# Head sums of a hybrid attention and recurrence layer: two float32r passes over high and low parts instead of one float32 product

## The chip, the core and the metric

The kernel runs on one core of a Trainium2 chip. The metric is the device time of one execution in microseconds (us). The core has a matmul engine (TensorE, "PE"), a vector engine (VectorE, "DVE"), a scalar engine for activation functions (ScalarE, "ACT"), GpSimd ("POOL") and SyncE ("SP"), which here issues the DMAs. Each works through its own queue in order; semaphores make one wait for another. Matmul results go to PSUM, all else lies in SBUF.

## What is computed

One layer over x of 512 positions by 1024 features, all in float32:

```
x = x + 0.5 * SwiGLU1(rmsnorm(x))            1024 -> 2816 -> 1024
p = rmsnorm(x) @ W_in
  q, k, v     8 heads of 64: stick-breaking attention, q and k rms-normalised per head,
              its output rms-normalised per head
  r, k, v, ..  8 heads of 64: RWKV-7 recurrence; its k is normalised per head, its output
              is group-normalised per head, plus the bonus sum(r * kf * r_k) * v
x = x + concat(o_sb, o_rw) @ W_out
x = x + 0.5 * SwiGLU2(rmsnorm(x))
```

Five times in it a sum over the 64 features of one head is wanted at every position: the mean square of q and of k (qm), the norm of the recurrence's k (kn), the bonus (bn), the variance of the recurrence's output (var), and the mean square of the attention's output (om).

## The kernel before

Features lie on the 128 partitions and the 512 positions along the free dimension, so that one [128, 512] tile holds a pair of heads. There are four pairs, j = 0 to 3, in the recurrence and four in the attention. Weights and activations are split into a float32r high part and a float32r rest, and `mm3` (L176) makes a float32 product of three float32r passes.

Three parts follow each other: FFN 1 (to about 370 us), the mixing stage, and FFN 2 (from about 763 us). The mixing stage has

- dense items on the shared list `stream` (L755): for each pair, projections K, R, V (recurrence) and Q (q or k of the attention), two SV for the attention's v; last PR(j), the output projection for pair j of both halves, eight groups of six matmuls each into "wo", added to x;
- three chains per pair. I(j), `rw_inverse`: blocks A, a small triangular inverse on VectorE with two trips through DRAM, three transposing blocks (tB, tA, W0), then seven products "inv" with copies between them, MG and N. C(j), `rw_chain`: six steps S, each waiting for the last; then y, the variance var, the gate g and the output orw. T(j), `att_core`: four steps of growing width (128 to 512), each z on PE, three activations per head, a scan and two other operations on VectorE, transposes wT, an exponential, and o; then the sum om.

A planner (L788) asks for these pieces in an order by estimated costs. The framework's scheduler then orders each engine's instructions by priority (C 3000, I 500, T none, L750) and by its own estimate of when inputs are ready. Tiles of one tag share a fixed number of buffers (`NB`, L97 for SBUF, `NM` for PSUM), which are handed out in the order in which the program asks for them: "r" has 10 and holds most of the recurrence's tiles; PSUM tag "mi" has 2 banks, used by I and by the y, var and g of C; "ma" has 3, used by T.

The sums over a head's 64 rows are made by `head_sum` (L200): a float32 matmul with the block matrix "blk" of the constants, which puts the sum over each head's rows on all of these rows. Its input is a square made by ScalarE (or the product `xr` for bn). There are 24: qm 8, kn 4, bn 4, om 4, var 4.

Of the kernel before, what the change touches and what calls it, by code (L numbers as in the profile page):

```python
# [16 lines left out]
F32 = mybir.dt.float32  # L17
# [65 lines left out]
def layer(ctx, tc, a, out, dbg=None):  # L83
# [10 lines left out]
        uid[0] += 1  # L94
        return f"{s}_{uid[0]}"

    NB = {"x": 16, "q": 3, "b": 4, "r": 10, "i": 10, "c": 6, "v": 4, "k": 4, "g": 8, "a": 4, "t": 2, "f": 4, "s": 2}  # L97
    NM = {"acc": 2, "sd": 1, "mi": 2, "ma": 3}
    NW = 3

# [47 lines left out]
    def cs(n):  # L148
        return cst[:, CST[n][0]:CST[n][1]]
# [47 lines left out]
    def norm_in(g):  # L197
        return [split(X[k], "x", v(g, k), "x") for k in range(KD)]

    def head_sum(ps, x):  # L200

        nc.tensor.matmul(ps, lhsT=cs("blk"), rhs=x, start=True, stop=True)

    def norm_scale(want_e=False, eng=nc.gpsimd):
        tot = None
# [136 lines left out]
    def eye():  # L342
        z = slot("i", "Z")
        nc.gpsimd.tensor_scalar(c3(z), cs("i64").unsqueeze(1).to_broadcast([P, NCH, CH]), 1.0, None, MUL)
        return z

    xs = norm_in("nmx")
    pwa = dense(a["wrw"][12], xs, "wa")
    S, rs, E = norm_scale(True)
# [56 lines left out]
    def item_k(j):  # L406

        ps = dense(a["wrw"][4 + j], xs, "k")
        yield
        xk = shifted(ps, 4 + j, "r", "xk")  # L410
        sq = slot("r", "ksq")
        act(sq, xk, AF.Square, scale=v("kk", j))
        pn = bank("sd", "kn")
        head_sum(pn, sq)
        nc.vector.tensor_scalar(sq, pn, 1e-24, None, MAX)
        act(sq, sq, AF.Ln)
        act(sq, sq, AF.Exp, scale=-0.5)
        kn = slot("r", "kkn")
        nc.vector.scalar_tensor_tensor(kn, xk, v("kk", j), sq, MUL, MUL)

        kf = slot("r", "kf")
        nc.vector.tensor_scalar(kf, av[j], v("ka", j), oka[:, j:j + 1], MUL, ADD)
        nc.vector.tensor_tensor(kf, kf, xk, MUL)
        ctxs[j] = dict(kn=kn, kf=kf)

    def item_r(j):

        ps = dense(a["wrw"][j], xs, "r")
        yield
        kn, kf = ctxs[j]["kn"], ctxs[j]["kf"]  # L430
        xr = shifted(ps, j, "r", "xr")
        Pd = slot("r", "Pd")
        act(Pd, Gs[j], AF.Exp, scale=-KAPPA)
        PC = small([P, NCH], "PC", 4)
        nc.gpsimd.tensor_scalar(PC.unsqueeze(2), c3(Pd)[:, :, CH - 1:CH], 1.0, None, MUL)
        AR = quad("AR")
        ar = c3(AR, P)
        nc.vector.scalar_tensor_tensor(ar[:, :, 1:CH], c3(kn)[:, :, 1:CH], -1.0, c3(Pd)[:, :, 0:CH - 1], MUL, MUL)
        nc.vector.tensor_scalar(ar[:, :, 0:1], c3(kn)[:, :, 0:1], -1.0, None, MUL)
        nc.vector.tensor_tensor(ar[:, :, CH:P], c3(xr), c3(Pd), MUL)  # L440
        nc.vector.scalar_tensor_tensor(xr, xr, v("rk", j), kf, MUL, MUL)
        pbn = bank("sd", "bn")
        head_sum(pbn, xr)
        bv = ctxs[j]["xv"]
        nc.vector.tensor_tensor(bv, pbn, bv, MUL)

        Pi = slot("r", "Pi")
        act(Pi, Gs[j], AF.Exp, scale=KAPPA)
        BK = quad("BK")
        bk = c3(BK, P)  # L450
        nc.vector.tensor_tensor(kn, kn, av[j], MUL)
        for src, q in ((kn, 0), (kf, 1)):
            for p, eng in ((0, nc.vector), (1, nc.gpsimd)):
                o_ = slice(CH * (q ^ p), CH * (q ^ p) + CH)
                eng.tensor_tensor(bk[rows[p], :, o_], c3(src[rows[p]]), c3(Pi[rows[p]]), MUL)
        ctxs[j].update(PC=PC, AR=AR, BK=BK, bv=bv)
# [153 lines left out]
    def rw_chain(j):  # L610

        js = slice(j * P, (j + 1) * P)
        PC, ar, ba, bv, UV, St = (ctxs[j][n] for n in ("PC", "ar", "ba", "bv", "UV", "St"))
        for c in range(1, NCH - 1):
            cc = slice(c * CH, (c + 1) * CH)
            nn = slice((c + 1) * CH, (c + 2) * CH)
            pS = bank("mi", "S", [P, CH])
            for p in range(2):
                nc.tensor.matmul(pS[rows[p]], lhsT=ar[rows[p], c, 0:CH], rhs=St[rows[p], cc], start=True, stop=True)
            nc.vector.scalar_tensor_tensor(St[:, nn], pS, PC[:, c:c + 1], St[:, nn], MUL, ADD)  # L620
            yield 1.2

        py = bank("mi", "y")
        for c in range(NCH):
            cc = slice(c * CH, (c + 1) * CH)
            for p in range(2):
                nc.tensor.matmul(py[rows[p], cc], lhsT=UV[p][:, cc], rhs=ba[p][:, c, CH:P], start=c == 0, stop=False)
        for c in range(1, NCH):
            cc = slice(c * CH, (c + 1) * CH)
            for p in range(2):  # L630
                nc.tensor.matmul(py[rows[p], cc], lhsT=St[rows[p], cc], rhs=ar[rows[p], c, CH:P],
                                 start=False, stop=c == NCH - 1)

        yc = slot("r", "yc")
        nc.scalar.copy(yc, py)
        yr = slot("r", "yr")
        act(yr, py, AF.Square)
        pv = bank("mi", "var")
        head_sum(pv, yr)
        act(yr, pv, AF.Ln, scale=1.0 / CH, bias=epsl)  # L640
        act(yr, yr, AF.Exp, scale=-0.5)
        nc.vector.scalar_tensor_tensor(yr, yc, v("lnw", j), yr, MUL, MUL)
        nc.vector.scalar_tensor_tensor(yr, yr, v("lnb", j), bv, ADD, ADD)
        pg = bank("mi", "g")
        nc.tensor.matmul(pg, lhsT=g2[:, js], rhs=sgx, start=True, stop=True)
        o = slot("g", "orw")
        nc.vector.tensor_tensor(o, pg, yr, MUL)
        outs[4 + j] = o
        yield 5
# [17 lines left out]
    def item_qk(j, e):  # L667

        ps = dense(a["wqk"][4 * e + j], xs, "qk"[e])
        yield  # L670
        qc = slot("k", "qc")
        nc.scalar.copy(qc, ps)
        ps = qc
        rn = slot("k", "rn")
        act(rn, ps, AF.Square, scale=CH ** -0.5)
        pm = bank("sd", "qm")
        head_sum(pm, rn)
        nc.vector.tensor_tensor(rn, pm, E, ADD)
        act(rn, rn, AF.Ln)
        act(rn, rn, AF.Exp, scale=-0.5)  # L680
        nc.vector.scalar_tensor_tensor(rn, ps, v("kn") if e else gq8, rn, MUL, MUL)
        ctxs["qk", j, e] = rn

    def att_core(j):
        qh, kh = ctxs["qk", j, 0], ctxs["qk", j, 1]
        po = bank("ma", "o")
        for i in range(4):
            L = (i + 1) * P
            pz = [bank("ma", "z") for _ in range(2)]
            for p in range(2):  # L690
                nc.tensor.matmul(pz[p][:, 0:L], lhsT=qh[rows[p], i * P:L], rhs=kh[rows[p], 0:L], start=True, stop=False)  # L691
            for p in range(2):
                nc.tensor.matmul(pz[p][:, i * P:L], lhsT=ninf, rhs=mkb, start=False, stop=True)
            ws = []
            for p in range(2):
                l = slot("a", "l")
                act(l[:, 0:L], pz[p][:, 0:L], AF.Abs)
                act(l[:, 0:L], l[:, 0:L], AF.Exp, scale=-1.0)
                act(l[:, 0:L], l[:, 0:L], AF.Ln, bias=1.0)
                r = slot("a", "r")  # L700
                nc.vector.tensor_scalar(r[:, 0:L], pz[p][:, 0:L], 0.0, None, MAX)
                nc.vector.tensor_tensor_scan(l[:, 0:L][:, ::-1], r[:, 0:L][:, ::-1], l[:, 0:L][:, ::-1], 0.0, ADD, ADD)
                nc.vector.tensor_tensor(r[:, 0:L], pz[p][:, 0:L], l[:, 0:L], SUB)
                ws.append(r)
            yield 2 + i
            ats = []
            for p in range(2):
                pt = bank("ma", "wT")
                for b in range(i + 1):
                    nc.tensor.transpose(pt[:, b * P:(b + 1) * P], ws[p][:, b * P:(b + 1) * P], cs("ident"))  # L710
                at = slot("t", "at")
                act(at[:, 0:L], pt[:, 0:L], AF.Exp)
                ats.append(at)
            for b in range(i + 1):
                for p in range(2):
                    hd = 2 * j + p
                    nc.tensor.matmul(po[rows[p], i * P:L], lhsT=Vt[b][:, hd * CH:(hd + 1) * CH],  # L717
                                     rhs=ats[p][:, b * P:(b + 1) * P], start=b == 0, stop=b == i)
            yield 2
        rn = slot("t", "orn")  # L720
        act(rn, po, AF.Square, scale=CH ** -0.5)
        pm = bank("ma", "om")
        head_sum(pm, rn)
        act(rn, pm, AF.Ln, bias=epsr)
        act(rn, rn, AF.Exp, scale=-0.5)
        o = slot("s", "osb")
        nc.vector.scalar_tensor_tensor(o, po, v("son", j), rn, MUL, MUL)
        outs[j] = o
        yield 4
# [146 lines left out]
```

## Time and profile before

| what | value |
|---|---|
| three timed runs | 1135.84, 1137.49, 1137.58 us |
| profiled execution, its own time | 1135.56 us |
| its span | 1133.8 us |
| PE busy | 1105.7 us (98%) |
| DVE, ACT, POOL busy | 567.3, 445.6, 182.6 us |

The span is what the profiler sees between the first and the last instruction; some 1.8 us lie around it. A matmul of 512 columns is listed with about 0.39 us, but these overlap: the next one starts 0.23 us later. So PE's busy time is read for gaps, not as work. A float32 matmul is two instructions in the trace, each 0.59 us when listed.

### The profile page before, as it was taken

Reading aid. Unit: us, or ns where it says so; the run is one execution under the profiler, and the core shown is the slowest. Engines: PE = TensorE matmul, PEld = TensorE weight load, DVE = VectorE, ACT = ScalarE, POOL = GpSimd, SP = SyncE. Lnnn points to the kernel's source line nnn. Section 1 sums busy time; section 2 is a strip of 40 time slices with the busy share of each in tenths; the row PEclk is TensorE's granted clock in tenths of the full one; section 3 lists DMA queues with packets and bytes.
Section 4 is the critical chain, followed back from the end, with each engine's and each line's share of the span. In section 5 each row is a group of like instructions: output and inputs, shape, how many; then the busy total and the mean of one; then the engine's idle time right before and its main releaser. Section 6 shows DMA issues by size and latency. Waiting matters only on the chain.

```text
span 1133.8 us, 16807 instructions
## 1 busy us (share of the span) xinstructions
PE 1105.7 (98%) x6499; PEld 870.7 (77%) x6499; DVE 567.3 (50%) x966; ACT 445.6 (39%) x782; POOL 182.6 (16%) x135
## 2 busy tenths in 40 slices
PE   8999999999999998999999998999999999999998
PEld 6888888888888766866677665777888888888887
DVE  7444443443333466487777777674434444433322
ACT  6333333333323553364644654553333333322221
POOL 1111111120001233221311312041111111110000
PEclk9999999999999999999999999998999999999999
DMA  5332333233333224311302102022333232334442
GB/s 203 100 96 93 102 93 102 93 90 102 99 93 104 90 66 112 88 47 40 75 27 53 39 23 57 11 74 93 93 101 96 94 102 93 103 90 116 115 114 68
DMA packets 67231, 97.79 MB, mean 86 GB/s; under 512 B 19280, under 2 KB 21456, under 8 KB 67152
## 3 DMA queue, kind: packets, MB, share of 16 engines
q1 hardware_dynamic: 67152, 96.73, 29.0%
q8 instruction: 51, 0.84, 0.3%
q14 instruction: 28, 0.23, 0.1%
HBM read 93.03 MB, written 3.67 MB: 85 GB/s over the span
## 4 chain that ended last, share of the span: by engine, by line
PE 87%; DVE 8%; ACT 2%; issue 1%; DMA 1%; SPq 0%; DVEq 0%; ACTq 0%
PE g L179 7%; PE g L178 7%; PE g L177 7%; PE dn L178 7%; PE dn L177 7%; PE u L179 7%; PE dn L179 7%; PE u L177 7%; PE u L178 7%; PE inv L566 2%; PE z L691 2%; PE o L717 1%; PE k L177 1%; PE k L179 1%; PE k L178 1%
## 5 line engine op out<-in xcount | busy, mean ns | idle before, releaser
L162 ACT CAST wh<-w 128x512 fp32r<-128x512 f32 (+1 forms) x315 | 192.1, 610 | 412.9 <-PE dn L178 146.6
L163 DVE TENSOR_TENSOR wl<-w,wh 128x512 fp32r<-128x512 f32 (+1 forms) x294 | 200.2, 681 | 246.4 <-ACT wh L162 245.7
L179 PE MATMUL g<-xh,wl 128*128 128x512 f32 x352 | 138.1, 392 | 1.9 <-DVE wl L163 1.9
L177 PE MATMUL u<-xh,wh 128*128 128x512 f32 x352 | 137.2, 390 | 2.6 <-ACT wh L162 2.6
L178 PE MATMUL g<-xl,wh 128*128 128x512 f32 x352 | 138.1, 392 | 0.7 <-DVE xl L193 0.7
L177 PE MATMUL g<-xh,wh 128*128 128x512 f32 x352 | 138.2, 393 | 0.1
L179 PE MATMUL u<-xh,wl 128*128 128x512 f32 x352 | 137.1, 390 | 0.0
L178 PE MATMUL u<-xl,wh 128*128 128x512 f32 x352 | 137.1, 389 | 0.0
L302 POOL TENSOR_TENSOR h<-sg,u 128x512 f32<-128x512 f32 x44 | 69.1, 1571 | 395.8 <-DVE u L300 386.2
L177 PE MATMUL dn<-hdh,wh 128*128 128x512 f32 x240 | 93.4, 389 | 0.0
L178 PE MATMUL dn<-hdl,wh 128*128 128x512 f32 x240 | 93.4, 389 | 0.0
L179 PE MATMUL dn<-hdh,wl 128*128 128x512 f32 x240 | 93.4, 389 | 0.0
L179 PEld LDWEIGHTS g<-xh,wl 128*128 128x128 f32 x352 | 66.8, 190 | 16.2 <-DVE wl L163 2.3
L177 PEld LDWEIGHTS u<-xh,wh 128*128 128x128 f32 x352 | 66.1, 188 | 17.1 <-ACT wh L162 3.3
L178 PEld LDWEIGHTS g<-xl,wh 128*128 128x128 f32 x352 | 66.6, 189 | 15.0 <-DVE xl L193 1.1
L177 PEld LDWEIGHTS g<-xh,wh 128*128 128x128 f32 x352 | 66.7, 189 | 14.7 <-ACT sq L134 0.5
L178 PEld LDWEIGHTS u<-xl,wh 128*128 128x128 f32 x352 | 66.2, 188 | 13.7
L179 PEld LDWEIGHTS u<-xh,wl 128*128 128x128 f32 x352 | 66.1, 188 | 13.6
L300 DVE TENSOR_TENSOR u<-u,S 128x512 f32<-128x512 f32 x44 | 30.4, 691 | 65.7 <-PE u L179 65.7
L163 POOL TENSOR_TENSOR wl<-w,wh 128x512 fp32r<-128x512 f32 x22 | 30.4, 1384 | 137.6 <-ACT wh L162 102.6
L177 PEld LDWEIGHTS dn<-hdh,wh 128*128 128x128 f32 x240 | 45.1, 188 | 9.4
L179 PEld LDWEIGHTS dn<-hdh,wl 128*128 128x128 f32 x240 | 45.1, 188 | 9.3
(268 smaller groups left out, 1798.6 us busy)
## 6 DMA issues: line engine op xcount, KB each, us to landing
w<-wgu SPq DMA_DIRECT2D x176, 256.0 KB, 2.6
w<-wd SPq DMA_DIRECT2D x80, 256.0 KB, 2.6
w<-wrw SPq DMA_DIRECT2D x28, 256.0 KB, 2.6
w<-wqk SPq DMA_DIRECT2D x16, 256.0 KB, 2.6
wv<-wv SPq DMA_DIRECT2D x16, 256.0 KB, 2.6
wo<-wo SPq DMA_DIRECT2D x16, 256.0 KB, 2.6
x<-xT SPq DMA_DIRECT2D x8, 256.0 KB, 5.4
w<-wd SPq DMA_DIRECT2D x16, 128.0 KB, 2.0
```

What stands on the lines that cost most here:

```text
L162: cp(hi[:, :n], raw[:, :n])
L163: pool.tensor_tensor(lo[:, :n], raw[:, :n], hi[:, :n].bitcast(F32), SUB)
L177: mms.append(nc.tensor.matmul(ps, lhsT=lh, rhs=rh, start=start, stop=False))
L178: nc.tensor.matmul(ps, lhsT=lh, rhs=rl, start=False, stop=False)
L179: nc.tensor.matmul(ps, lhsT=ll, rhs=rh, start=False, stop=stop)
L300: nc.vector.tensor_tensor(u, pu, S, MUL)
L302: nc.gpsimd.tensor_tensor(h, sg, u, MUL)
L566: nc.tensor.matmul(ps[rows[p], cc], lhsT=l_[rows[p], cc], rhs=r[rows[p], cc], start=True, stop=True)
L691: nc.tensor.matmul(pz[p][:, 0:L], lhsT=qh[rows[p], i * P:L], rhs=kh[rows[p], 0:L], start=True, stop=False)
L717: nc.tensor.matmul(po[rows[p], i * P:L], lhsT=Vt[b][:, hd * CH:(hd + 1) * CH], rhs=ats[p][:, b * P:(b + 1) * P], start=b == 0, stop=b == i)
```

## The change

Every head sum takes a rounded copy of its input (`hi`, float32r), the exact rest (`lo`, made on GpSimd), and two float32r matmuls into the same bank. For the four kinds that sum a square, ScalarE computes the square twice, once in float32 and once rounded to float32r; for bn it copies. The block matrix is copied once to a float32r tile. The two parts live in a new tag "h" of two buffers; tag "r" goes from 10 buffers to 8. The variance now squares the copy yc in SBUF instead of y in PSUM.

```diff
-    NB = {"x": 16, "q": 3, "b": 4, "r": 10, "i": 10, ... "s": 2}
+    NB = {"x": 16, "q": 3, "b": 4, "r": 8, "i": 10, ... "s": 2, "h": 2}
...
-    def head_sum(ps, x):
-
-        nc.tensor.matmul(ps, lhsT=cs("blk"), rhs=x, start=True, stop=True)
+    def head_sum(ps, x, again):
+
+        hi = slot("h", "hsh", F32R)
+        again(hi)
+        lo = slot("h", "hsl", F32R)
+        nc.gpsimd.tensor_tensor(lo, x, hi.bitcast(F32), SUB)
+        nc.tensor.matmul(ps, lhsT=blk, rhs=hi, start=True, stop=False)
+        nc.tensor.matmul(ps, lhsT=blk, rhs=lo, start=False, stop=True)
+
+    def square_sum(ps, src, tag, s, scale=1.0):
+
+        x = slot(tag, s)
+        act(x, src, AF.Square, scale=scale)
+        head_sum(ps, x, lambda hi: act(hi, src, AF.Square, scale=scale))
+        return x
...
+    blk = pc.tile([P, P], F32R, name="blk")
+    nc.vector.tensor_copy(blk, cs("blk"))
...
-        head_sum(pbn, xr)
+        head_sum(pbn, xr, lambda hi: nc.scalar.copy(hi, xr))
...
-        yr = slot("r", "yr")
-        act(yr, py, AF.Square)
         pv = bank("mi", "var")
-        head_sum(pv, yr)
+        yr = square_sum(pv, yc, "r", "yr")
...
-        rn = slot("t", "orn")
-        act(rn, po, AF.Square, scale=CH ** -0.5)
         pm = bank("ma", "om")
-        head_sum(pm, rn)
+        rn = square_sum(pm, po, "t", "orn", CH ** -0.5)
```

The items Q and K are changed in the same way.

The number at the end of a name counts tiles in the order in which the program asks for them. On PE before, the variance of pair 1 (var_5993) stands among the dense matmuls of the last q, Q(3, 0) (q_5305), and pair 2's inverse (inv_6103) begins right behind it:

```order
L177 MATMUL q_5305<-xh_2934,wh_5326 128x512
L178 MATMUL q_5305<-xl_2935,wh_5326 128x512
L179 MATMUL q_5305<-xh_2934,wl_5327 128x512
L710 MATMUL wT_5166<-cst,r_5154 128x128 x2
L177 MATMUL q_5305<-xh_2938,wh_5326 128x512
L178 MATMUL q_5305<-xl_2939,wh_5326 128x512
L202 MATMUL var_5993<-yr_5991,cst 128x512
L645 MATMUL g_5999<-sgx_3077,g_617_2902 128x512
L566 MATMUL inv_6103<-X_6099,Aa_5725 64x64
```

In the changed kernel the same variance (var_6098, now two matmuls) stands behind the sum of attention 3 (om_5941), and pair 2's inverse (inv_6215) behind that:

```order
L206 MATMUL om_5941<-hsh_5944,blk 128x512
L207 MATMUL om_5941<-hsl_5946,blk 128x512
L206 MATMUL var_6098<-hsh_6101,blk 128x512
L655 MATMUL g_6111<-sgx_3079,g_617_2902 128x512
L207 MATMUL var_6098<-hsl_6103,blk 128x512
L578 MATMUL inv_6215<-X_6211,Aa_5827 64x64
L578 MATMUL inv_6215<-X_6211,Aa_5828 64x64
```

All dense items but the last three PR come before these rows; in the kernel before, the last dense item, Q(3, 1), and all four PR came after them. On ACT the copy of y (yc_6096) is made early, but the rounded square of it (hsh_6101) waits for the sum of attention 3 (hsh_5944):

```order
L134 ACTIVATE at_5920<-wT_5915 128x512
L134 ACTIVATE at_5927<-wT_5922 128x512
L134 ACTIVATE orn_5942<-o_5695 128x512
L134 ACTIVATE hsh_5944<-o_5695 128x512
L134 ACTIVATE hsh_6101<-yc_6096 128x512
L134 ACTIVATE orn_5942<-om_5941,epsr 128x512
L134 ACTIVATE orn_5942<-orn_5942 128x512
L134 ACTIVATE yr_6099<-var_6098,epsl 128x512
```

The copy yc_6096 stands 60-odd rows further up on ACT. At the end of the mixing stage, before, the variance of pair 3 (var_6818) lies between output matmuls of PR1 (wo_6523, wo_6531) and of attention 3:

```order
L179 MATMUL wo_6523<-osh_6491,wol_6520 128x512
L202 MATMUL var_6818<-yr_6816,cst 128x512
L645 MATMUL g_6824<-sgx_3077,g_617_2902 128x512
L710 MATMUL wT_5820<-cst,r_5805 128x128 x4
L717 MATMUL o_5593<-at_5818,Vt_3566 64x128
L177 MATMUL wo_6531<-orh_6487,woh_6519 128x512
```

Now it (var_6933) stands between pair 3's own y (y_6900) and PR3 (wo_7060), which needs it:

```order
L643 MATMUL y_6900<-AR_5433,St_6874 64x64 x14
L206 MATMUL var_6933<-hsh_6936,blk 128x512
L655 MATMUL g_6946<-sgx_3079,g_617_2902 128x512
L207 MATMUL var_6933<-hsl_6938,blk 128x512
L177 MATMUL wo_7060<-orh_7046,woh_7056 128x512
```

No dense matmul is left between the first product of pair 3's inverse and this place.

## Rows read from the trace of the kernel before

**Rows 1.** the page's first lines: span, and PE busy, its share, its instructions

```profile
span 1133.8 us, 16807 instructions
PE 1105.7 (98%) x6499; PEld 870.7 (77%) x6499; DVE 567.3 (50%) x966; ACT 445.6 (39%) x782; POOL 182.6 (16%) x135
```

**Rows 2.** busy time by stretch: PE, PEld, DVE, ACT, POOL, PE clock, DMA

```profile
400.00:687.00 287.00, 271.17 (x2537) 194.32 (x2535) 203.05 (x403) 152.20 (x288) 71.04 (x57) 0.99 0.22 58
687.00:763.30 76.30, 74.29 (x630) 53.98 (x630) 53.03 (x85) 37.42 (x74) 17.02 (x12) 0.98 0.18 48
```

**Rows 3.** the chain of waits around a head sum: start, us, what

```profile
404.63 0.23 PE v L179
404.86 0.86 PE qm L202 x2
```

**Rows 4.** groups by shape, POOL, 400:770 us: busy, mean ns, idle before

```profile
L163 POOL TENSOR_TENSOR wl<-w,wh 128x512 fp32r<-128x512 f32 x17 | 24.0, 1413 | 119.4 <-ACT wh L162 92.4 <-PE q L179 8.9 <-PE q L178 6.9
```

**Rows 5.** timeline of PE, attention 1, z of three steps: start, us

```profile
550.53 0.49 PE L691 MATMUL z<-rn,rn 64*128 64x128 f32 x4
555.72 0.70 PE L691 MATMUL z<-rn,rn 64*128 64x256 f32 x4
562.36 0.92 PE L691 MATMUL z<-rn,rn 64*128 64x384 f32 x4
```

**Rows 6.** timeline, ACT and DVE, attention 3 ending and variance 3

```profile
721.29 0.60 ACT L134 ACTIVATE l<-z 128x512 f32<-128x512 f32 x1 [3.88 <-PE z L693]
...
727.21 0.59 ACT L635 COPY yc<-y 128x512 f32<-128x512 f32 x1 [1.82 <-PE y L631]
729.58 0.69 ACT L134 ACTIVATE yr<-var,epsl 128x512 f32<-128x512 f32 x1 [0.79 <-PE var L202]
733.14 0.60 ACT L134 ACTIVATE orn<-o 128x512 f32<-128x512 f32 x1 [1.67 <-PE o L717]
734.34 0.61 ACT L189 CAST orh<-orw 128x512 fp32r<-128x512 f32 x1
734.99 1.42 DVE L190 TENSOR_TENSOR orl<-orw,orh 128x512 fp32r<-128x512 f32 x1 [0.24 <-ACT orh L189]
```

**Rows 7.** timelines and a group: inverse 0, pair 3 S, y, then A

```profile
465.98 1.15 PE L566 MATMUL inv<-X,Aa 64*64 64x64 f32 x32
479.34 1.09 PE L596 MATMUL MG<-BA,Q 64*64 64x128 f32 x16
482.45 0.33 PE L619 MATMUL S<-St,AR 64*64 64x64 f32 x4
...
718.61 0.28 DVE L620 SCALAR_TENSOR_TENSOR St<-S,PC,St 128x64 f32<-128x64 f32 x1 [1.31 <-PE S L619]
719.46 0.28 DVE L620 SCALAR_TENSOR_TENSOR St<-S,PC,St 128x64 f32<-128x64 f32 x1 [0.56 <-PE S L619]
725.06 1.15 PE L627 MATMUL y<-BA,UV 128*64 128x64 f32 x30
...
L489 PE MATMUL A<-AR,BK 64*128 64x128 f32 x128 | 13.2, 298 | 3.8 <-DVE BK L455 2.7 <-DVE BA L492 0.7 <-DVE St L620 0.4
```

**Rows 8.** timelines of POOL, DVE and PE: pair 3, from tA to inverse

```profile
667.77 1.77 POOL L529 TENSOR_SCALAR AR<-cst 128x512 f32<-128x512 f32 x1 [22.40 <-PE tA L518]
696.50 1.27 DVE L553 TENSOR_TENSOR X<-G,cst 128x512 f32<-128x512 f32 x2
697.22 1.15 PE L566 MATMUL inv<-X,Aa 64*64 64x64 f32 x32
```

**Rows 9.** timeline of PE: first z of attention 3, last output matmul

```profile
687.06 0.49 PE L691 MATMUL z<-rn,rn 64*128 64x128 f32 x4
762.77 0.40 PE L179 MATMUL wo<-osh,wol 128*128 128x512 f32 x1
```

**Rows 10.** busy time by stretch, around 428 us, columns as in rows 2

```profile
426.00:428.00 2.00, 0.39 (x6) 0.39 (x8) 2.00 (x3) 0.62 (x1) 0.41 (x1) 1.00 0.71 185
428.00:430.00 2.00, 2.00 (x16) 1.68 (x15) 0.94 (x4) 0.00 (x0) 0.00 (x0) 0.53 0.59 134
```

More of the change, by code (lines that the diff above doesn't have):

```diff
@@ L95, in nm @@
         return f"{s}_{uid[0]}"
-    NB = {"x": 16, "q": 3, "b": 4, "r": 10, "i": 10, "c": 6, "v": 4, "k": 4, "g": 8, "a": 4, "t": 2, "f": 4, "s": 2}
+    NB = {"x": 16, "q": 3, "b": 4, "r": 8, "i": 10, "c": 6, "v": 4, "k": 4, "g": 8, "a": 4, "t": 2, "f": 4, "s": 2, "h": 2}
     NM = {"acc": 2, "sd": 1, "mi": 2, "ma": 3}
@@ L410, in item_k @@
         xk = shifted(ps, 4 + j, "r", "xk")
-        sq = slot("r", "ksq")
-        act(sq, xk, AF.Square, scale=v("kk", j))
         pn = bank("sd", "kn")
-        head_sum(pn, sq)
+        sq = square_sum(pn, xk, "r", "ksq", v("kk", j))
         nc.vector.tensor_scalar(sq, pn, 1e-24, None, MAX)
@@ L673, in item_qk @@
         ps = qc
-        rn = slot("k", "rn")
-        act(rn, ps, AF.Square, scale=CH ** -0.5)
         pm = bank("sd", "qm")
-        head_sum(pm, rn)
+        rn = square_sum(pm, ps, "k", "rn", CH ** -0.5)
         nc.vector.tensor_tensor(rn, pm, E, ADD)
@@ L719, in att_core @@
             yield 2
-        rn = slot("t", "orn")
-        act(rn, po, AF.Square, scale=CH ** -0.5)
         pm = bank("ma", "om")
-        head_sum(pm, rn)
+        rn = square_sum(pm, po, "t", "orn", CH ** -0.5)
         act(rn, pm, AF.Ln, bias=epsr)
```

## The prediction

> **What bounds the kernel now.** The page comes first: TensorE (PE) is counted busy for 1105.7 of 1133.8 us [rows 1]. The two FFNs at the ends do not contain the change; everything that moves lies in the mixing stage, about 370 to 763 us. The busy time by stretch shows that PE has little slack there too: 15.8 us idle from 400 to 687 us, and 2.0 us from 687 us, where attention 3 begins, to 763 us [rows 2]. PE is kept busy because the long serial chains (I = inverse, C = chain, T = attention, one of each per head pair j) are laid beside dense projections. A chain step alone leaves PE idle; it is free only while dense work stands next to it in PE's order. So I read the order next, and the chains' own step times after that.
>
> **The passes themselves.** One float32 head sum holds PE for 0.86 us, against 0.23 us from one float32r matmul to the next [rows 3]. Two float32r passes take 0.45 us, so each of the 24 sums frees 0.41 us: 24 x 0.41 = 9.8 us. That is all there is to gain.
>
> **What each sum gets in addition.** One more ScalarE pass (0.60 us, the Square of orn [rows 6]) and a GpSimd subtraction (1.41 us, the mean of the same operation for the weights [rows 4]) stand between the input and the second pass: some 2.0 us more of latency per sum, 14 us on ScalarE and 34 us on GpSimd. Neither engine is near its limit (152 and 71 us busy of 287 [rows 2]), so as plain load I cost them at nothing where dense work stands beside the sum. The one copy of blk on VectorE is nothing.
>
> **What the order does.** This is the term that decides. The two parts of a sum take both buffers of the new tag "h", and those are handed out in the order in which the program asks for them. Thus only one head sum can be in flight, and none can pass an earlier one in the program. The program asks for pair 1's variance after attention 3's. In the kernel before, the scheduler put that variance far ahead; now it stands right behind attention 3's last sum. (With the buffers of "r" cut to 8 and nothing else changed, the sums keep the order of before but for neighbours, so it is "h" that does this.) The variance had already taken one of the two PSUM banks "mi" that the inverses use too. So I2, C2, I3 and C3 fall behind T3, when all projections are used up. What is left to cover them is the output projection (PR1 to PR3), and that waits for these very chains.
>
> I work out the stretch from T3's first z to the last output-projection matmul, as it now stands in PE's order.
> 1. T3 alone. The first two steps take 5.2 and 6.6 us from z to z [rows 5]; the third is taken as 8.5, between these and the last. The last takes 2.1 for its two z, then from the first ScalarE step on z (721.3) to the end of o (733.1) 11.8 us [rows 6], from which I take off 1.7 for VectorE's other work in it: 10.1. Sum 32.5.
> 2. T3's last sum: 0.6 + 0.6 + 1.4 + 0.4 = 3.0. Pair 1's sum then gets its buffers: another 1.4 + 0.4 and semaphores. Sum 5.0.
> 3. From that variance to PR1's first matmul: in before 729.6 to about 735.7, the end of orl, the first half of the 1.42 us row [rows 6], 6.1; now the first inverse products stand in between: 7.
> 4. I2 to pair 3's second A block, with 21 output matmuls: 21 x 0.23 = 4.8, three products at 1.08 are 3.2, two MG and N at about 1.05 are 3.1, A 3.3 (13.2 for four pairs) [rows 7], 0.3 for S, 3 of waits for VectorE: 17.7.
> 5. To pair 3's tA block, with five S steps that depend on each other: 9.
> 6. From tA to the first product of I3. The reset of AR on GpSimd starts at 667.8, I3's products at 697.2: 29.4 us [rows 8]. VectorE's X pair is held by other work for about 3 of it. I take 27; C2's variance and all of PR2 (10.9) lie inside.
> 7. I3 with nothing beside it: the first inverse took 465.98 to 482.45 = 16.5 with some dense matmuls in the way [rows 7]; I take 14. Six S at 0.85 (718.61 to 719.46): 5.1. y from 725.06 to yc at 727.2: 2.1 [rows 6, 7].
> 8. y to PR3: yc at 727.2 to the end of orl at 735.7 is 8.5 [rows 6]; plus 0.6 and 1.4, less 0.4: 10.1. PR3: 48 x 0.23 = 10.9.
>
> Sum 140.4, where before needs 687.06 to 763.0 = 75.9 [rows 9]: +64.5. Against it, T3 begins earlier, since what is now behind it is no longer before it: two variances with their g (3.4), I2's products, MG and N (10.7), six S and y (4.1), I3's A (3.3) and its three blocks of 16 small matmuls, taken as a product each (3.2), are 24.7 us [rows 3, 7]. 20 of the 24 sums are done by then (20 x 0.41 = 8.2), and 15 more output matmuls (3.4). That is 29.5 earlier; new waits of PE on the serial sums, as in om, qm, var, kn of one row (about 1.9 us apart at least, with 1 to 1.5 of other work between), take back some 4 (bounds -4 and +12). Start: -25.5.
>
> **The clock.** PE is counted busy for 0.39 us of 426 to 428, and the granted clock is then 0.53 over the next two us, which is nearly all at the lower of its two levels, 1.2 GHz [rows 10]. Steps 1, 2, 7 and 8 leave PE idle for more than half. On their paths lie about 6 us of matmuls in T3, 8 of products, and the first matmuls after each gap; I take half of such work at half clock: +6 (bounds 0 and 25). The Trainium skill ("TensorE: Matmul & The Clock Gate", section "HAM oscillation — how this bites in real kernels") says that idle between groups of matmuls sends the engine back to half rate each time. The trace agrees at this place; by the rule in full every uncovered group would run slow, which is the third rival.
>
> Net: 64.5 - 25.5 + 6 = +45.0. The profiled execution took 1135.56 us, 1.9 below the median of 1137.49 and 0.3 below the lowest of the three runs; 1135.6 + 45.0 = 1180.6, in round numbers 1181.
>
> **Bounds.** Tail 122 (T3 steps at 28, I3 as 11, step 6 fully beside PR2) to 156 (T3 as contended as before, step 6 at 29.4, 3 us more per variance); start -33 to -17; clock 0 to 25. Two ends that fall together give 1148 and 1212.
>
> **Rivals.** *The passes are what counts.* If dense work still hid all chains, the kernel would be faster by the 9.8: 1126. For it: PE busy 98% [rows 1], and the chains were hidden before. Against it: PE's order has no dense matmul between T3's last steps, nor between I3's first product and C3's variance. It decides only if those stretches total less than 10 us, and T3's steps alone are more. Chance 4%.
> *Latency, not order.* Each sum delays its reader by 2.0 us and PE has nothing to put there: 24 x 2.0 - 9.8 = +38, 1174, spread evenly over 400 to 763. For it: POOL's queue is in order, with waits for weight casts in it. Against it: in the first half, dense matmuls stand between a sum's input and its passes. Chance 8%.
> *The clock stays down from T3 on.* The exposed matmuls (T3 6, products 16, S and y 8) and about half of the 35 us of output matmuls run at half rate: +30 to +45 in place of 6, some 1205 to 1215. For it: rows 10. Against it: the mean granted clock from 687 to 763 is 0.98 in spite of such gaps [rows 2], and PR1 to PR3 are dense runs. Chance 12%.
> *The chains are shortened by emptier engines*, as nothing competes in the tail: tail 122, 1155 to 1160. Chance 13%, in my range.
>
> **Numbers.** My forecast of 1181, give or take 15, has 63%. 0.2% (2.3 us) is about what can be told from no change. Faster 4%, within 0.2% 1%, slower 95%. The range of 1150 to 1212 leaves out the first rival and the far end of the third.
>
> **What would show it.** Right: 400 to about 660 loses nothing (T3's first z near 660, not 687); then PE is busy for about 60% up to about 805, with idle that ends on ACT (var, z), POOL (hsl) and VectorE; head-sum passes of about 0.23 each; granted clock under 1.0 in several places after T3. Wrong: idle spread evenly from 400 on (second rival), or T3's first z later than 680, or dense matmuls at 1.2 GHz throughout PR1 and PR3.

## The result and the profile after

The changed kernel takes 1201.68 us (median of four runs, 1198.35 to 1207.72) against 1136.8: a ratio of 1.0577, 95% interval 1.0534 to 1.062. The forecast was 1181, in a range of 1150 to 1212. The sign and the main mechanism, the order of the sums, came out as forecast. The sum is 18 us short in the profiled execution (1198.35 against 1180.6): 14.7 of them lie in the start of T3, which the forecast had 25.5 us earlier, and 3.5 in the tail behind it. The profiled execution's page:

```profile
span 1196.5 us, 16875 instructions
PE 1126.3 (94%) x6499; PEld 884.5 (74%) x6499; DVE 574.5 (48%) x967; ACT 457.9 (38%) x806; POOL 211.7 (18%) x159
PEclk9999999999999999999899958887999999999999
```

The span is 62.7 us longer [rows 1], and the row of the clock, in 40 slices of 29.9 us, has a 5, three 8 and a 7 at 688 to 838 us, and one more 8 at 568 to 598 us; before has a single 8 in the whole row. The timeline of PE around T3 and at the end of the mixing stage:

```profile
676.26 0.49 PE L699 MATMUL z<-rn,rn 64*128 64x128 f32 x4 [1.34 <-DVE rn L689]
...
711.88 2.72 PE L725 MATMUL o<-at,Vt 128*64 128x128 f32 x16
715.84 0.50 PE L206 MATMUL om<-hsh,blk 128*128 128x512 f32 x1 [1.23 <-ACT hsh L134]
717.18 0.50 PE L207 MATMUL om<-hsl,blk 128*128 128x512 f32 x1 [0.85 <-POOL hsl L205]
717.84 0.61 PE L206 MATMUL var<-hsh,blk 128*128 128x512 f32 x1 [0.16 <-ACT hsh L134]
719.20 1.39 PE L207 MATMUL var<-hsl,blk 128*128 128x512 f32 x1
729.31 0.49 PE L177 MATMUL wo<-orh,woh 128*128 128x512 f32 x1
...
812.22 0.79 PE L177 MATMUL wo<-orh,woh 128*128 128x512 f32 x1 [4.46 <-ACT orh L189]
825.90 0.40 PE L179 MATMUL wo<-osh,wol 128*128 128x512 f32 x1
```

Pair 1's variance now follows T3's sum by 2 us, and I2, C2, I3, C3 come after it. From T3's first z to the start of the last output matmul there are 149.6 us, where before had 687.06 to 762.77, 75.7 [rows 9]: +73.9. T3 itself begins only 10.8 us earlier. That is the whole difference in two numbers, 73.9 - 10.8 = 63.1, where the spans differ by 62.7. Busy time by stretch (the columns of rows 2: length, busy time of PE, PEld, DVE, ACT, POOL, then PE clock):

```profile
400.00:676.20 276.20, 252.32 (x2063) 181.47 (x2062) 190.41 (x347) 151.09 (x289) 92.43 (x73) 0.97 0.22 60
676.20:714.70 38.50, 25.62 (x96) 13.43 (x96) 16.32 (x29) 13.99 (x33) 1.27 (x1) 0.60 0.05 14
676.20:826.30 150.10, 115.13 (x1102) 81.27 (x1102) 72.47 (x142) 50.61 (x95) 23.50 (x19) 0.77 0.09 24
```

Before, PE was idle for 2.0 of the last 76 us at clock 0.98 [rows 2]; now for 35 of 150 us at 0.77. It is busy for 77% of 676 to 805 us, where the forecast had about 60%; a matmul at the lower clock is counted busy for longer (a z product of T3's last step for 2.07 us, with the clock up in e9 for 1.12). In the stretch ahead of T3 its idle time rose from 15.8 us [rows 2] to 23.9. What PE waited for in the tail (engine, line, what it waited for: us, times, longest):

```profile
PE wT L718 <- DVE r L711: 11.5, 4, 4.4
PE wo L177 <- ACT orh L189: 10.3, 2, 5.9
PE var L206 <- ACT hsh L134: 2.0, 2, 1.9
```

These are steps of a chain that nothing covers: attention waits for VectorE's scan, the first matmuls of PR2 and PR3 for what is made of a variance.

### The profile page after: what moved, and what is told of

Same layout as the page of the kernel before. It is cut to its first block, busy times and chain, and to the rows that moved or that the text cites. A ratio compares the mean times of both kernels' runs of the same rounds, so it can differ in the third digit from the quotient of the medians.

```text
span 1196.5 us, 16875 instructions
## 1 busy us (share of the span) xinstructions
PE 1126.3 (94%) x6499; PEld 884.5 (74%) x6499; DVE 574.5 (48%) x967; ACT 457.9 (38%) x806; POOL 211.7 (18%) x159
## 4 chain that ended last, share of the span: by engine, by line
PE 83%; DVE 9%; ACT 3%; issue 2%; POOL 1%; DMA 0%; SPq 0%; DVEq 0%; POOLq 0%; ACTq 0%
PE g L179 7%; PE g L178 7%; PE dn L179 7%; PE u L177 7%; PE g L177 7%; PE dn L177 7%; PE dn L178 7%; PE u L179 7%; PE u L178 7%; PE inv L578 2%; PE z L699 2%; DVE G L548 2%; PE o L725 2%; DVE l L710 1%; PE k L179 1%
## 5 line engine op out<-in xcount | busy, mean ns | idle before, releaser
L177 PEld LDWEIGHTS u<-xh,wh 128*128 128x128 f32 x352 | 66.1, 188 | 15.8 <-ACT wh L162 2.1
L179 PEld LDWEIGHTS u<-xh,wl 128*128 128x128 f32 x352 | 66.1, 188 | 13.9
L178 PEld LDWEIGHTS dn<-hdl,wh 128*128 128x128 f32 x240 | 45.1, 188 | 9.4
```

What stands on the lines that cost most here:

```text
L177: mms.append(nc.tensor.matmul(ps, lhsT=lh, rhs=rh, start=start, stop=False))
L178: nc.tensor.matmul(ps, lhsT=lh, rhs=rl, start=False, stop=False)
L179: nc.tensor.matmul(ps, lhsT=ll, rhs=rh, start=False, stop=stop)
```

## The experiments

All times are medians in us; every ratio is against runs of the kernel before on the same chip.

| run | order of the sums | low part on | us | ratio, 95% |
|---|---|---|---|---|
| after | shared "h" | GpSimd | 1201.7 | 1.0577 (1.0534 to 1.062) |
| e1 order alone | shared "h" | none, float32 | 1181.1 | 1.0394 (1.0365 to 1.0423) |
| e2 var own | var free | GpSimd | 1151.5 | 1.0139 (1.0103 to 1.0174) |
| e3 four buffers | shared "h" | GpSimd | 1210.1 | 1.0643 (1.0605 to 1.0681) |
| e4 r eight | as before | none, float32 | 1140.3 | 1.0029 (1.0012 to 1.0046) |
| e5 low part on DVE | shared "h" | VectorE | 1183.0 | 1.0427 (1.039 to 1.0463) |
| e6 var own, DVE | var free | VectorE | 1131.9 | 0.996 (0.9942 to 0.9979) |
| e7 qm, kn only | var, om, bn free | GpSimd | 1139.9 | 1.004 (1.0015 to 1.0065) |
| e8 T3 filled | shared "h" | GpSimd | 1200.6 | 1.0577 (1.0546 to 1.0608) |
| e9 T3 covered | shared "h" | GpSimd | 1189.9 | 1.0468 (1.0439 to 1.0497) |
| e10 om own, DVE | om free | VectorE | 1150.7 | 1.0116 (1.0095 to 1.0138) |
| e11 var in r, DVE | var free | VectorE | 1136.1 | 0.9993 (0.9976 to 1.001) |
| e12 qm, kn, DVE | var, om, bn free | VectorE | 1136.9 | 0.9992 (0.9975 to 1.001) |

**Is it the order, or the passes? (e1, e2, e4)** e1 keeps the shared tag and takes the passes away:

```diff
-        hi = slot("h", "hsh", F32R)
+        hi = slot("h", "hsh")
         again(hi)
-        lo = slot("h", "hsl", F32R)
-        nc.gpsimd.tensor_tensor(lo, x, hi.bitcast(F32), SUB)
-        nc.tensor.matmul(ps, lhsT=blk, rhs=hi, start=True, stop=False)
-        nc.tensor.matmul(ps, lhsT=blk, rhs=lo, start=False, stop=True)
+        nc.tensor.matmul(ps, lhsT=cs("blk"), rhs=hi, start=True, stop=True)
```

> The float32 product of before, one per head sum, but its operand is a square (or product) written once more by ScalarE into one of two buffers that all kinds of head sum share; no GpSimd subtraction, no second pass. The shared buffers bring TensorE the order of the changed kernel (pair 1's variance behind the output norm of T3). Theory, order: 1190 to 1212 us, tail after T3's first score product over 140 us. Rival, latency of two passes and the GpSimd subtraction: 1133 to 1145 us, since neither is here. Rival, the clock: as the order theory, but only if the sparse stretch is there.

Measured 1181.1, +44.5 over before. The order makes the larger part; GpSimd's step and the second pass are absent here and can make none of it. (e1 keeps two other things of the change: one more ScalarE pass per sum, and the eight buffers of "r", which cost 3.8 by e4 below.) The time lies below the theory's 1190 to 1212, since that took the passes for a gain that would be missing here. The timeline of PE in e1:

```profile
661.03 0.49 PE L696 MATMUL z<-rn,rn 64*128 64x128 f32 x4
...
702.25 1.91 PE L204 MATMUL var<-hsh,cst 128*128 128x512 f32 x2
...
806.70 0.39 PE L179 MATMUL wo<-osh,wol 128*128 128x512 f32 x1
```

T3 begins at 661.0, and 145.7 us follow. That the forecast put T3 at 661.6 is luck: it had counted in a gain from the passes that e1 does not have. The passes cost 20.6 us more under this order by the medians, 18.7 by the profiled spans; T3 begins 15.2 later with them (676.26 - 661.03), and the tail is 3.9 longer. Of the 15.2, some 2 are not lost: the changed kernel has 36 output matmuls ahead of T3, e1 27 (and before 21), 0.23 us each.

e2 keeps the passes and lets the variance go: its parts come from tag "i", the ten buffers of the inverse's steps (`ht` is a new argument of `square_sum` and `head_sum` for the tag of the two parts).

```diff
-        yr = square_sum(pv, yc, "r", "yr")
+        yr = square_sum(pv, yc, "r", "yr", ht="i")
```

> The changed kernel with its two float32r passes, but the variance's high and low parts taken from the ten buffers of the inverse's steps and not from the two shared ones; pairs 0 to 2's variances stand before the last attention core's output norm again. Theory, order: 1120 to 1140 us (before less up to 9.8 us of passes, plus some waits), tail under 90 us. Rival, latency of the two passes: 1174 to 1200 us, since each sum still waits for ScalarE and GpSimd.

1151.5: 50 us of the 65 come back, more than any price of the passes, and yet the time is 11 us above the theory's range. The tail is 70.2 us (709.63 to 779.79). What is left lies ahead of T3; the rows of e2 for GpSimd and PE show one place of it:

```profile
574.17 1.41 POOL L205 TENSOR_TENSOR hsl<-xr,hsh 128x512 fp32r<-128x512 f32 x1 [2.25 <-issue]
575.66 1.61 POOL L467 TENSOR_TENSOR BK<-kkn,Pi 64x512 f32<-64x512 f32 x1
577.34 1.59 POOL L163 TENSOR_TENSOR wl<-w,wh 128x512 fp32r<-128x512 f32 x1
578.90 1.71 POOL L205 TENSOR_TENSOR hsl<-yr,hsh 128x512 fp32r<-128x512 f32 x1
```

```profile
572.79 0.40 PE L206 MATMUL var<-hsh,blk 128*128 128x512 f32 x1
580.66 0.49 PE L207 MATMUL var<-hsl,blk 128*128 128x512 f32 x1 [3.33 <-POOL hsl L205]
```

The variance's low part is the fourth in GpSimd's queue and comes 7.9 us after the high part; PE stands still for 3.3 of them.

e4 is the kernel before with one number changed:

```diff
-    NB = {"x": 16, "q": 3, "b": 4, "r": 10, ... "s": 2}
+    NB = {"x": 16, "q": 3, "b": 4, "r": 8, ... "s": 2}
```

> The kernel before with eight instead of ten buffers of the receptance class, nothing else. TensorE's order is nearly that of before. Theory, order: 1134 to 1142 us. Rival, the two buffers taken from that class are what costs: over 1160 us.

1140.3, +3.8 by the medians: small, as expected, and contained in all runs here that keep eight.

**Too few buffers? (e3)** Four shared buffers and, to make room, eight for the inverse:

```diff
-    NB = {"x": 16, "q": 3, "b": 4, "r": 8, "i": 10, ... "s": 2, "h": 2}
+    NB = {"x": 16, "q": 3, "b": 4, "r": 8, "i": 8, ... "s": 2, "h": 4}
```

> The changed kernel with four shared buffers for the head sums' parts (two sums at a time) instead of two, and eight instead of ten for the inverse's steps. They are still handed out in the order of the program, so pair 1's variance still stands behind T3's output norm. Theory, order: 1190 to 1212 us, as the changed kernel. Rival, two buffers are too few: 1130 to 1155 us.

1210.1, as the order theory has it. In e3 pair 1's variance still stands behind T3's sum:

```profile
723.24 0.49 PE L206 MATMUL om<-hsh,blk 128*128 128x512 f32 x1 [1.23 <-ACT hsh L134]
...
724.92 0.43 PE L206 MATMUL var<-hsh,blk 128*128 128x512 f32 x1
```

Four buffers in place of two do not change here who may pass whom; more than four were not tried. The 8 us on top do not come from the sums: the first head sum begins at 414.80 instead of 405.17, so they were lost ahead of it. The first FFN's hidden tiles take buffers of "i" too, which may be why; that was not followed up.

**Which sums must be free? (e10, e11)** e10 frees only attention's output norm, e11 only the variance, as e6 below does. Both subtract on VectorE. First e10's line, then e11's:

```diff
-        rn = square_sum(pm, po, "t", "orn", CH ** -0.5)
+        rn = square_sum(pm, po, "t", "orn", CH ** -0.5, "a")
...
-        yr = square_sum(pv, yc, "r", "yr")
+        yr = square_sum(pv, yc, "r", "yr", ht="r")
```

> As the changed kernel with the subtraction on VectorE (1183.0 us), but the parts of attention's output norm (4 of 24 sums) come from the four buffers of attention's own class. Pair 1's variance and pair 2's inverse then stand ahead of T3's first score product or beside it; pair 3's inverse and variance are still behind T3. Theory, order, every inverse behind T3 costs: half of the way to the free order, 1145 to 1168 us. Rival, once pair 1's variance is free all is won: 1130 to 1140 us. Rival, the tag of the output norm does not matter: 1179 to 1187 us.

> As e6 (1131.9 us: variance's parts out of the shared tag, subtraction on VectorE), but they come from the eight buffers of the receptance class instead of the inverse's ten. The variances of pairs 0 to 2 stand ahead of the last attention core's output norm as in e6. Theory, order: 1129 to 1138 us. Rival, which buffers they take costs as much as the order: 1142 us or more.

e10 (1150.7) stands between e5 and e6, as forecast when one inverse of two is left behind T3. From its T3 (661.29) to its last output matmul (777.37) are 116.1 us. Two stretches of e10, split at the end of T3's sum:

```profile
661.30:716.00 54.70, 50.77 (x563) 36.36 (x563) 39.59 (x94) 27.01 (x58) 4.40 (x5) 0.97 0.11 27
716.00:777.80 61.80, 52.56 (x502) 39.75 (x500) 35.14 (x56) 22.06 (x37) 14.22 (x10) 0.89 0.17 43
```

T3 with I2 beside it runs at clock 0.97, and PE idles for 3.9 of 54.7 us; behind it, with I3 and C3, for 9.2 of 61.8. e11 is within its forecast; why it is 4 us above e6 was not tried (T3 begins at 677.67 in e11 and at 691.24 in e6, so more than the variance's place differs).

That the inverse falls behind T3 together with the variance because of the PSUM tag "mi" is argued from the program; no run gave "mi" another bank.

**What makes the passes dear? (e5, e6, e7, e12)** e5 is the changed kernel, e6 is e2, with one edit:

```diff
-        nc.gpsimd.tensor_tensor(lo, x, hi.bitcast(F32), SUB)
+        nc.vector.tensor_tensor(lo, x, hi.bitcast(F32), SUB)
```

> The changed kernel with the subtraction for the low part on VectorE instead of GpSimd; TensorE's order of the sums is that of the changed kernel. In the changed kernel TensorE waits 2.1 us at 571 for bn's low part behind two other operations in GpSimd's queue, and runs at half clock for the next 11 us; against the kernel with the order alone 8 us are lost there. Theory, GpSimd's queue and the clock drop behind it make up half of what the passes cost: 1186 to 1196 us, no clock drop at 574 to 585. Rival, the length of the subtraction counts for nothing: 1199 to 1205 us. Rival, VectorE, for which TensorE waits most in T3, becomes later still: 1203 to 1212 us.

> The kernel with the variance's parts in the inverse's buffers (1151.5 us), with the subtraction on VectorE. There the low part of two variances came 7.9 and 5.6 us after the high part, behind other GpSimd work, and the granted clock fell once. Theory, with the order free only GpSimd's queue is left as a cost: 1132 to 1143 us. Rival, every sum is late by its second step wherever that runs: 1149 to 1156 us.

Both gain 17 to 20 us (18.7 and 19.6 by the medians, 17.1 and 20.4 by the ratios); e5 is 3 us below its theory's range, e6 at the lower end of its own. The group of the subtraction, first in the changed kernel, then in e5 (min, median, max ns):

```profile
L205 POOL TENSOR_TENSOR hsl<-rn,hsh x8: 1273/1287/1357, 389.9 to 670.6; 128x512 fp32r<-128x512 f32 x8
```

```profile
L205 DVE TENSOR_TENSOR hsl<-rn,hsh x8: 673/688/821, 389.6 to 653.5; 128x512 fp32r<-128x512 f32 x8
```

In e5 the gain lies wholly ahead of T3, which begins at 658.57 instead of 676.26, 17.7 us earlier; the tail is 150.8 against 149.6. A difference of 0.6 us in the 20 subtractions ahead of T3 is 12 us even if all of it were bare, and PE's waits for low parts there add up to some 6 us in the changed kernel. So the shorter operation alone can't make it; what one late part sets off comes on top. In the changed kernel (GpSimd, then PE):

```profile
569.36 1.89 POOL L467 TENSOR_TENSOR BK<-kkn,Pi 64x512 f32<-64x512 f32 x1 [1.23 <-ACT l L134]
571.33 1.79 POOL L205 TENSOR_TENSOR hsl<-xr,hsh 128x512 fp32r<-128x512 f32 x1
```

```profile
570.42 0.40 PE L206 MATMUL bn<-hsh,blk 128*128 128x512 f32 x1
570.65 0.39 PE L178 MATMUL k<-xl,wh 128*128 128x512 f32 x1
573.17 0.50 PE L207 MATMUL bn<-hsl,blk 128*128 128x512 f32 x1 [2.13 <-POOL hsl L205]
...
576.97 2.07 PE L699 MATMUL z<-rn,rn 64*128 64x512 f32 x2
```

```profile
572.00:576.00 4.00, 2.83 (x11) 1.92 (x12) 2.36 (x5) 1.63 (x3) 2.01 (x2) 0.84 0.02 4
576.00:580.00 4.00, 4.00 (x15) 1.97 (x14) 1.76 (x2) 0.49 (x1) 0.61 (x1) 0.50 0.39 127
580.00:584.00 4.00, 4.00 (x11) 1.90 (x9) 0.24 (x1) 1.12 (x2) 0.00 (x0) 0.50 0.01 4
```

bn's low part waits behind BK, PE waits 2.13 us for it with dense work of K queued behind, and then the granted clock is 0.50, the lower of the two levels, for all of 576 to 584 (with its edges some 10 us, not the 11 of e5's expectation): a z product of two instructions takes 2.07 us, in e1 1.12. Between the sums qm at 559.88 and om at 596.40 the changed kernel needs 36.5 us, e1 (556.12 and 584.21) 28.1. Of these 8.4 us, 2.3 are ten more matmuls of V that stand there in the changed kernel (23 against 13); some 6 are lost at this one place. In e5 the clock is 1.00 from 555 to 590, and T3 begins 2.5 us ahead of e1. That GpSimd's queue and the clock behind it make the passes dear is shown at this place and in e2 above; the rest of e5's 17.7 us was not traced.

The Trainium skill ("GPSIMD Engine Reference", section "4.1 Engine selection") sends elementwise work on two inputs to VectorE and puts GpSimd at about half its speed; the rows agree (1287 against 688 ns).

e7 and e12 use passes only for qm and kn, the other sums keep the float32 product; e12 subtracts on VectorE.

```diff
...
+        if not two:
+            nc.tensor.matmul(ps, lhsT=cs("blk"), rhs=x, start=True, stop=True)
+            return x
...
```

> Two float32r passes for the 12 sums of the dense items Q and K alone (qm, kn; shared tag of two buffers, low part on GpSimd); bn, om and var keep the float32 product and no shared buffer. The variances stand as far ahead as before. Theory, where dense matmuls stand beside a sum its latency is hidden and the pass gain shows: 1140.3 (eight buffers of the receptance class) less 12 x 0.41 = 1135, 1131 to 1139 us. Rival, latency counts everywhere: 1144 to 1156 us.

> As e7 (1139.9 us: passes for the 12 sums qm and kn alone), with the subtraction on VectorE. Theory, GpSimd's queue ate the gain of 12 x 0.41 us in e7: 1131 to 1137 us. Rival, GpSimd was not the reason: 1138 to 1143 us.

e7 gives 1139.9, between the two forecasts and 1 us above the theory's: nothing won on e4's 1140.3. e12 gives 1136.9, so of the 4.9 us that 12 sums free, 3 to 4 arrive once GpSimd is out of the way. With all 24 sums and the variance free, e6 is some 8 us under e4, of 9.8 freed, but e11 only 4. The price of a pass, 0.41 us less per sum, is in accord with e6 and e12 as an upper bound; no run has it alone.

**What does the clock cost in T3? (e8, e9)** Both add float32 matmuls whose results are thrown away. e8 puts them in front of the transposes; they write the transposes' bank and so wait for VectorE as well. e9 puts them behind the score products, into a bank of their own. First e8, then e9:

```diff
                 pt = bank("ma", "wT")
+                if j == 3 and p == 0:
+                    for _ in range(3):
+                        nc.tensor.matmul(pt, lhsT=g2[:, 0:P], rhs=sgx, start=True, stop=True)
...
+            if j == 3:
+                pj = bank("sd", "junk")
+                for _ in range(i + 2):
+                    follow(nc.tensor.matmul(pj, lhsT=g2[:, 0:P], rhs=sgx, start=True, stop=True), zl)
```

(`zl` is the step's last score matmul; `follow` only keeps the order.)

> The changed kernel with three more float32 matmuls of 512 columns (0.86 us each at full clock, results thrown away) ahead of the first transposes of each of T3's four steps, where TensorE waits for VectorE. Theory, T3 is stretched by the half clock (38.3 us instead of 32.5): the clock stays up through most of T3, T3 takes 32 to 36 us although 10 us of work are added, total 1194 to 1199 us. Rival, T3's length is that of ScalarE's and VectorE's steps: clock up, T3 38 us or more, total 1201 to 1210 us.

> The changed kernel with 2, 3, 4 and 5 float32 matmuls of 512 columns (0.86 us each at full clock, results thrown away, into a bank that nothing else uses then) right behind the four steps' score products of T3, so that they run while TensorE waits for VectorE (2.8 to 4.4 us a step); the matmuls of e8 waited for VectorE themselves. The sums keep the changed kernel's order. Theory, half clock stretches T3 by some 6 us: clock near 1.0 in T3, T3 31 to 35 us from its first score product to the end of its output instead of 38.3, total 1192 to 1198 us. Rival, T3's length is ScalarE's and VectorE's: clock up, T3 37 to 40 us, total 1199 to 1205 us.

e8 tells little: its matmuls stand in the chain, not beside it. In its last two steps they start at the lower clock, 5.46 and 5.28 us for three; T3 takes 41.2 us, as its rival has it, and the total stays (1200.6). e9 answers. Timeline of PE and the stretch of T3 in e9:

```profile
674.79 0.49 PE L699 MATMUL z<-rn,rn 64*128 64x128 f32 x4 [1.28 <-DVE rn L689]
...
693.77 1.12 PE L699 MATMUL z<-rn,rn 64*128 64x512 f32 x2
...
704.62 1.09 PE L729 MATMUL o<-at,Vt 128*64 128x128 f32 x14
```

```profile
674.70:705.80 31.10, 29.18 (x124) 14.24 (x124) 16.51 (x29) 13.89 (x33) 0.97 (x1) 1.00 0.04 9
```

With 14 useless products (12 us) T3 takes 30.9 us (to 705.71) instead of 38.3, at clock 1.00 instead of 0.60, and the kernel gains 11.8 us by the medians, 8.8 by the profiled spans; at 1189.9 it is 2 us below the theory's range. The clock is the cause of T3's length: ScalarE and VectorE are busy for the same time in both (14.0 and 16.3 us before the filling, 13.9 and 16.5 with it). T3 bare of the lower clock is 1.6 us shorter than the 32.5 of the forecast.

## Why the prediction was right, and where its sum was off

| term | forecast | changed kernel | what the runs say |
|---|---|---|---|
| start of T3 | -25.5 | -10.8 | e1: -26.0; e5: -28.5 |
| 1. T3 | 32.5 | 38.3 | e9: 30.9 at full clock |
| 2. T3's sum, pair 1's sum | 5.0 | 6.0 | |
| 3. variance to PR1 | 7 | 8.7 | |
| 4. to pair 3's second A | 17.7 | 15.4 | |
| 5. to tA | 9 | 8.1 | |
| 6. tA to I3 | 27 | 27.8 | |
| 7. I3, S, y | 21.2 | 23.1 | |
| 8. y to PR3, PR3 | 21.0 | 22.4 | |
| clock | +6 | in the steps | |

**The order decides: right, and shown.** e1 and e2 part it from the passes, e10 grades it. The first rival, "The passes are what counts", fell: a gain of up to 8 us exists (e6), but 41 to 45 us of order stand against it (e1, with and without the 3.8 of e4). The ScalarE pass that e1 keeps is not the cause: e6 has it too.

**The tail: right to 3.5 us** (149.9 by its steps, with the last matmul's own time, against 146.4 with the clock). Steps 2 to 8 are built from rows of before and miss by 2.3 at most. That T3 was taken too long and the clock's cost too small cancels in part: T3 alone loses 7.4 us to the lower level, where +6 was set for all. The forecast counted only the matmuls of T3 that it held exposed. The granted clock of T3 is 0.60 bare and 1.00 covered; PR3's first matmuls are 0.43 us apart, and 0.23 some 5 us after it begins. The Trainium skill's rule of the forecast ("TensorE: Matmul & The Clock Gate", section "HAM oscillation — how this bites in real kernels": idle between groups sends the engine back to half rate each time) is borne out by T3 from its second step on (0.50 from 684 to 714), and by the first matmuls of PR2 and PR3; I3's products from 780 to 796, with waits of 0.4 to 0.9 us between them, run at 1.00.

**The start of T3: the step that failed.** It came at -10.8 instead of -25.5, outside the forecast's own bounds of -33 to -17. The forecast's -25.5 has two parts. The first is the order: -24.7 for the work that moves behind T3 and +3.4 for 15 output matmuls that move ahead of it, -21.3. e1 has -26.0 with 6 more output matmuls than before, which makes -24.0 with 15: 2.7 us better than forecast. The second is the passes, -8.2 for what they free and 4 for new waits, -4.2. Measured, from e1 to the changed kernel, it is +15.2, or +13.2 without the nine output matmuls: 17.4 us worse. What failed there is "as plain load I cost them at nothing where dense work stands beside the sum", and the 4 us of waits set in its place. GpSimd is indeed busy for only a third of that stretch (92 of 276 us); but the low part stands in a queue behind BK and weight parts, PE's own order lets nothing pass the second pass, and a stop of 2.1 us was followed by half clock for 10 us. On VectorE the same term is -2.5 (e5 against e1), or -5.9 without the 15 output matmuls more that e5 has ahead of T3; the forecast's -4.2 lies between. That cost was in the forecast as the second rival's argument ("POOL's queue is in order") and was weighed as 2.0 us times 24, evenly spread. It is not even: it sits where GpSimd has other work.

**The range.** It held with 10 us to spare; that the order saved more than forecast is luck, and hides 2.7 of the 17.4 us. Its ends do not follow from its bounds in one way. The three lower bounds together give 1149, near the 1148 that stands, but the three upper ones give 1224 and not 1212; and 45 in place of 6 for the clock gives the third rival 1220, not 1215.

**The rivals.** Latency, as put, fell: e1 loses 44.5 us without GpSimd's step, and the sums of e6 are all late by a second step, a shorter one on VectorE, and it is the fastest of all. What is left of it are the passes' 20.6 us on GpSimd, about half of the 38 it had. The clock staying down from T3 on has the nearer total (1205), for a part of its reasons: T3 runs at half rate for 30 of its 38 us, the output projections mostly do not. The forecast's own sign of error, T3 later than 680, did not show, but 676 is not the "near 660" that it named as right.

**Open:** e3's loss ahead of the first head sum, e11's 4 us over e6, the part of the passes' cost ahead of T3 that is not at 570 to 585, and step 3 (1.7 us over the forecast). What the lower clock costs behind T3 was not isolated.

**A better version:** e6, 1131.9 us, 0.996 of before (0.9942 to 0.9979): the variance's parts out of the shared tag, the subtraction on VectorE.

## What to carry to other kernels

A buffer tag that several kinds of work share is a queue: buffers are handed out in the order of the program, and what the program asks for last stands last, however early it is ready; four buffers in place of two did not change that here. So before giving steps a common tag, look which of them the scheduler had let pass one another. And price an engine's work by what stands ahead of it in that engine's queue, not by that engine's share of busy time; where TensorE then waits, add what its clock takes afterwards.

## What the runs showed that was not expected

- A single wait of 2.13 us inside dense work is followed by granted clock 0.50 over 576 to 584 us, though PE is counted busy for all of these 8 us.
- Useless work made the kernel faster: 14 matmuls in PE's waits took 7.4 us off T3 (38.3 to 30.9) and brought the clock from 0.60 to 1.00.
- More buffers made it slower: 1210.1 us with four shared ones, for two taken from another class; the cause stays open.
